# FFN-out of a hybrid decoder layer in one core: more units computed by Strassen products, operands loaded twice

## The chip, the core and the metric

One core of a Trainium2 chip runs the whole layer as one program. The engines are TensorE (PE, with its weight loads PEld shown apart), VectorE (DVE), ScalarE (ACT), GpSimd (POOL) and SyncE (SP, which here only issues transfers). The metric is the device time of one execution in microseconds (us). The time before is 2707.65 us, the median of three runs (2701.99 to 2710.27).

## The reference, cut to what matters

The layer takes x of 512 tokens by 2048 channels in float32. The part that the change is about is the feed-forward block and what follows it:

```python
h = rmsnorm(x, ffn_norm_g[i])
hid = h @ w_ffn_in[i]                                  # 2048 -> 2 x 5632
x = x + (silu(hid[..., :5632]) * hid[..., 5632:]) @ w_ffn_out[i]   # 5632 -> 2048
x = x + sigmoid(rmsnorm(x, ple_norm_g[i]) @ w_ple_gate[i]) * (p[i] @ w_ple[i])
```

Before it stand the combined projection, gated spatial mixing, stick-breaking attention and the output projection w_o.

## The kernel before

**Numbers.** Each float32 operand is split in a high part (rounded by ACT) and a low part (DVE subtracts the high one), and a product takes three matmuls: high x high, high x low, low x high (mm3, L269 to L273).

**Units and columns.** An operand *unit* is 256 channels by 512 tokens: two halves of the channels by two halves of the tokens, four blocks of [128, 256]. An output *column* (called a pair in the code, L744) is 256 channels by 512 tokens. A unit is multiplied in one of two ways.

- Plain (P): four weight blocks by two token rows, 12 matmuls of 512 columns.
- Strassen (S): seven products by sums of blocks (PRODUCTS, L52), 21 matmuls of 256 columns. It needs seven operand blocks (three as they are, four sums) and seven weight blocks (three and four in the same way). Outputs are mixed from PSUM by ACT and DVE (mix, L646). Two S units whose weights lie side by side share their weight preparation (a *double*, L402); a unit left over is a *single*.

In the stage before, FFN-in, the products are doubled: the high and low operand parts stand side by side, so that an S unit is 7 matmuls of 512 and 7 of 256 columns (L620 to L632). FFN-out does not use this.

**Weights.** A ring of four landing places and three slots (whi, wlo) holds them. For a P double one transfer of 512 KB is issued by SP (L314). For an S double SP issues 256 KB (the first block twice, L316) and 384 KB (L318), then POOL issues 256 KB that are added onto what has landed (L338); DVE adds two more sums (L350), ACT makes the high parts of 5 + 2 blocks (L334), DVE the low parts (L331). A landing place goes to the next weights once the low parts are made, so SP's issue of weights goes at the pace of DVE.

**The order.** Python emits the program unit by unit; a clock ticks once per P unit and twice per S double (tick, L198). At a tick a first load of a coming operand may be issued (fetch, at most one, among the next three), a form may be begun, and waiting steps go on. Manual dependencies hold what a tick emits in its place among the units.

**FFN-out.** The hidden vector is 22 units in DRAM. They don't fit at once, so there are three passes, each over all eight output columns (L1347): 8, 7 and 7 units, of the kinds in PASSES (L33), SSSSSPPP, SSSSSPP and SSSPPPP. The first pass writes its columns to DRAM as sums, the second adds to them (loads and stores 512 KB per column), the third adds, scales, adds the residual x1, writes x2, and sums squares for the next norm. In a pass's first column all units are multiplied plainly, since a plain product needs only the four blocks themselves. After the last column use of a unit its place is free for the next pass.

**Late forms.** An S operand that comes from DRAM is built by late_form (L509) and plain_first (L487): one load of 512 KB, the four blocks split, and at once the four sums, which stay in 4 KB of scratch per partition; one block's sum takes the place of a plain block and so waits until the plain column has used it. The gate stage after FFN-out (GATE = SSSSSPPP over x2) and FFN-in (over x1) use the same forms. There are eight places for S operands.

Of the kernel before, what the change touches and what calls it, by code (L numbers as in the profile page):

```python
# [32 lines left out]
PASSES = "SSSSSPPP", "SSSSSPP", "SSSPPPP"  # L33
# [18 lines left out]
PRODUCTS = (1, 0), (5, 5), (4, 1), (3, 4), (0, 6), (2, 2), (6, 3)  # L52
# [13 lines left out]
def hybrid_layer(  # L66
# [120 lines left out]
    builds = deque()  # L187
# [10 lines left out]
    def tick():  # L198
# [70 lines left out]
    def mm3(ps, sh, sl, mh, ml, start, stop, halved=False):  # L269
        for s in (slice(0, 256), slice(256, T)) if halved else (slice(None),):  # L270
            nc.tensor.matmul(ps[:, s], sh, mh[:, s], start=start, stop=False)  # L271
# [148 lines left out]
    class Form(Staged):  # L420


        def __init__(self, kind, steps, sizes, ready, src=None, far=False):
# [3 lines left out]
            self.src, self.there, self.block, self.due = src, not far, None, 0  # L427

# [6 lines left out]

        def raw(self):
# [3 lines left out]
        def get(self):  # L440
            if self in builds:
                builds.remove(self)
            return super().get()
# [43 lines left out]
    def plain_first(form, raw):  # L487
# [5 lines left out]
        for out, p, q, op in ((t[:, 0], b[:, 1], b[:, 0], ALU.subtract),  # L493
                              (v.f(), b[:, 1], b[:, 3], ALU.subtract),
                              (t[:, 1], t[:, 0], b[:, 3], ALU.subtract),
                              (t[:, 2], t[:, 1], b[:, 2], ALU.add)):
            nc.vector.tensor_tensor(out=out, in0=p, in1=q, op=op)  # L497
        give(raw)
        form.at_plain = True
        yield  # L500
# [5 lines left out]
        split_into(x[:, 1, 0], x[:, 1, 1], v.f())  # L506
        give(v)

    def late_form(src, ready=always, gain=None, far=False):  # L509
# [3 lines left out]
        def steps(form):  # L513
# [5 lines left out]
            yield from plain_first(form, w)  # L519
            return form.operand()  # L520

        return Form("S", steps, [(parts, 2 * PLACE, "place")] + [(wholes, 1024, "low")] * 2, ready,
                    src, far)

    def strassen_form(src, ready=always, gain=None, raw=PLACE):


        def steps(form):
            w = src()
            form.blocks = (parts.take(2 * PLACE, "place"),)  # L530
            if gain:
# [3 lines left out]
            nc.vector.tensor_tensor(out=b[:, 4], in0=b[:, 1], in1=b[:, 0], op=ALU.subtract)  # L535
            nc.vector.tensor_tensor(out=b[:, 1:6:4], in0=b[:, 1:5:3],
                                    in1=b[:, 3:4].to_broadcast([P, 2, 256]), op=ALU.subtract)
# [950 lines left out]
```

## Time and profile before

| | |
|---|---|
| median of three runs | 2707.65 us |
| the profiled execution | 2701.99 us, of which the span from first to last instruction is 2701.9 us |
| FFN-in, 44 columns | about 1175 to 2047 us in the span |
| FFN-out, passes 1, 2, 3 | about 2049 to 2214, 2214 to 2364, 2364 to 2510 us |
| gate stage | about 2520 to 2702 us |
| DVE, ACT, POOL busy over the span | 79%, 51%, 17% |

The stages' edges are read from the matmuls: in FFN-out an S unit shows as matmuls of 256 columns and a P unit as matmuls of 512. The views used are the profile's page, groups of instructions by line and shape within a stretch, windows (busy time of each engine in a stretch, granted clock, busy share of the 16 DMA engines), waits, the timeline, and the transfers of one tensor. A mean duration of an instruction includes the time in which the next one has already begun, so for matmuls the pace is taken from windows and not from durations.

### The profile page before, as it was taken

The numbers are of one execution on the slowest core, as the hardware profiler recorded it, in microseconds if no ns is written. First come the engines' busy times: TensorE is split into PE (matmuls) and PEld (weight loads), VectorE is DVE, ScalarE is ACT, GpSimd is POOL, SyncE is SP. The second block draws the span as 40 slices with busy tenths as digits, with TensorE's granted clock in tenths as the row PEclk, the third lists the DMA queues.
The fourth block names the chain that finished last, engine by engine and source line by source line (L and its number), as shares of the span: only waits on it lengthen the run. The fifth ranks groups of instructions, "written<-read, shape, count | busy, mean of one in ns | idle before, by whom it ended". The sixth has DMA issues, their size and how long they took to land.

```text
span 2701.9 us, 43167 instructions
## 1 busy us (share of the span) xinstructions
PE 2668.1 (99%) x15875; PEld 2354.6 (87%) x15875; DVE 2147.0 (79%) x3621; ACT 1367.3 (51%) x2143; POOL 459.0 (17%) x543
## 2 busy tenths in 40 slices
PE   8999999999999999999999999999999999999999
PEld 6888888989998889988888888888888999988898
DVE  7687878787887566688988888888889667688776
ACT  7656565655554343374444444444445344453543
POOL 0232323232220000001111111111111111110110
PEclk9999999999999999999999999999999999999999
DMA  7677777777776467678888888888887668688784
GB/s 224 156 185 175 181 173 186 170 187 197 177 186 197 140 173 200 173 219 211 212 212 202 200 203 205 201 198 210 195 210 206 181 167 262 184 249 236 218 243 133
DMA packets 303268, 529.40 MB, mean 196 GB/s; under 512 B 25680, under 2 KB 162896, under 8 KB 303056
## 3 DMA queue, kind: packets, MB, share of 16 engines
q1 hardware_dynamic: 242304, 426.22, 49.9%
q0 software_dynamic: 60752, 100.43, 23.8%
q8 instruction: 124, 2.03, 0.3%
q14 instruction: 88, 0.72, 0.1%
HBM read 479.36 MB, written 47.19 MB: 195 GB/s over the span
## 4 chain that ended last, share of the span: by engine, by line
PE 88%; DVE 5%; DMA 2%; ACT 2%; issue 1%; POOL 1%; SPq 0%; DVEq 0%; ACTq 0%; POOLq 0%
PE ps L629 39%; PE ps L272 14%; PE ps L273 14%; PE ps L271 14%; PE small L629 4%; DVE wlo L331 2%; DVE out L688 1%; PE small L1084 1%; PE small L959 1%; ACT whi L334 1%; DMA wholes<-w_in 0%; DMA wholes<-w_first 0%; DVE wholes L350 0%; PE small L1034 0%; DVE parts L267 0%
## 5 line engine op out<-in xcount | busy, mean ns | idle before, releaser
L334 ACT ACTIVATE whi<-wholes 128x512 fp32r<-128x512 f32 (+4 forms) x950 | 857.6, 917 | 838.3 <-DVE wholes L350 261.9
L629 PE MATMUL ps<-parts,whi 128*128 128x512 f32 x3384 | 1134.8, 398 | 0.3 <-DVE p L688 0.3
L331 DVE TENSOR_TENSOR wlo<-wholes,whi 128x512 fp32r<-128x512 f32 (+4 forms) x950 | 962.4, 1046 | 101.0 <-ACT whi L334 100.5
L271 PE MATMUL ps<-parts,whi 128*128 128x256 f32 (+1 forms) x2675 | 855.1, 323 | 15.7 <-ACT parts L266 9.7
L272 PE MATMUL ps<-parts,whi 128*128 128x256 f32 (+1 forms) x2640 | 857.0, 325 | 1.0 <-DVE parts L267 0.8
L273 PE MATMUL ps<-parts,wlo 128*128 128x256 f32 (+1 forms) x2640 | 855.9, 325 | 0.9 <-DVE wlo L331 0.9
L629 PEld LDWEIGHTS ps<-parts,wlo 128*128 128x128 f32 x3384 | 635.8, 188 | 142.6 <-issue 1.0
L629 PE MATMUL ps<-parts,wlo 128*128 128x256 f32 x3384 | 671.1, 279 | 0.0
L271 PEld LDWEIGHTS ps<-parts,whi 128*128 128x128 f32 x2675 | 508.8, 190 | 60.7 <-ACT parts L266 10.8
L629 PEld LDWEIGHTS ps<-parts,whi 128*128 128x128 f32 x3384 | 545.3, 189 | 5.0 <-issue 1.0
L272 PEld LDWEIGHTS ps<-parts,whi 128*128 128x128 f32 x2640 | 502.7, 191 | 47.2 <-DVE parts L267 2.8
L273 PEld LDWEIGHTS ps<-parts,wlo 128*128 128x128 f32 x2640 | 502.7, 191 | 41.2 <-DVE wlo L331 2.8
L350 DVE TENSOR_TENSOR wholes<-wholes 128x256 f32<-128x256 f32 (+1 forms) x794 | 326.8, 412 | 21.8 <-DMA wholes<-w_ffn_out 4.0
L338 POOL DMA_DIRECT2D wholes<-w_ffn_in x172 | 149.7, 871 | 693.0 <-DVE wholes L350 238.8
L688 DVE TENSOR_TENSOR out<-out,ps 128x256 f32<-128x256 f32 x388 | 160.3, 415 | 131.7 <-ACT out L685 131.5
L338 POOL DMA_DIRECT2D wholes<-w_in x132 | 118.0, 895 | 486.1 <-DVE wholes L350 145.7
L655 DVE TENSOR_TENSOR out<-out 128x256 f32<-128x256 f32 x144 | 60.9, 423 | 114.7 <-ACT out L652 112.2
L629 PE MATMUL small<-parts,whi 128*128 128x512 f32 x344 | 136.5, 397 | 0.0
L267 DVE TENSOR_TENSOR parts<-wholes,parts 128x1024 fp32r<-128x1024 f32 (+4 forms) x131 | 123.7, 950 | 14.9 <-ACT parts L266 14.5
L266 ACT ACTIVATE parts<-wholes 128x1024 fp32r<-128x1024 f32 (+4 forms) x131 | 105.8, 834 | 42.0 <-DVE wholes L497 20.0
L338 POOL DMA_DIRECT2D wholes<-w_ffn_out x56 | 56.9, 1020 | 403.4 <-DMA wholes<-w_ffn_out 139.6
L1328 ACT ACTIVATE out<-out 128x512 f32<-128x512 f32 x44 | 27.8, 633 | 157.9 <-DVE out L1327 157.9
(121 smaller groups left out, 1655.0 us busy)
## 6 DMA issues: line engine op xcount, KB each, us to landing
wholes<-w_ffn_in SPq DMA_DIRECT2D x172, 384.0 KB, 5.6
wholes<-w_in SPq DMA_DIRECT2D x132, 384.0 KB, 4.9
wholes<-w_ffn_in SPq DMA_DIRECT2D x172, 256.0 KB, 4.8
wholes<-w_ffn_in POOLq DMA_DIRECT2D x172, 256.0 KB, 5.4
wholes<-w_in SPq DMA_DIRECT2D x132, 256.0 KB, 4.2
wholes<-w_in POOLq DMA_DIRECT2D x132, 256.0 KB, 5.0
wholes<-x SPq DMA_DIRECT2D x33, 512.0 KB, 5.5
wholes<-w_ffn_out SPq DMA_DIRECT2D x31, 512.0 KB, 4.5
```

The lines of the kernel that those rows point to most:

```text
L266: return (nc.scalar.activation(hi, src, AF.Copy), nc.vector.tensor_tensor(out=lo, in0=src, in1=hi.bitcast(F32), op=ALU.subtract))
L267: nc.vector.tensor_tensor(out=lo, in0=src, in1=hi.bitcast(F32), op=ALU.subtract))
L271: nc.tensor.matmul(ps[:, s], sh, mh[:, s], start=start, stop=False)
L272: nc.tensor.matmul(ps, sh, ml, start=False, stop=False)
L273: return nc.tensor.matmul(ps, sl, mh, start=False, stop=stop)
L331: in_turn(nc.vector.tensor_tensor(out=self.lo[:, blocks], in0=r, in1=h.bitcast(F32), op=ALU.subtract))
L334: in_turn(nc.scalar.activation(h, r, AF.Copy))
L338: nc.gpsimd.dma_start(out=raw[:, 3:5], in_=self.src[:, 1:3], accum_op=ALU.add)
L350: in_turn(nc.vector.tensor_tensor(out=o, in0=x, in1=y, op=ALU.add))
L629: m = nc.tensor.matmul(out, l, r, start=first and k == 0, stop=last and k == 1)
L655: in_turn(nc.vector.tensor_tensor(out=out, in0=x, in1=y, op=op))
L688: in_turn(nc.vector.tensor_tensor(out=out, in0=x, in1=y, op=op))
```

## The change

1. PASSES becomes the sizes 8, 7, 7. All 22 units of FFN-out are built as S operands. PLAIN_UNTIL says in how many first columns the unit at each place of a pass is still multiplied plainly: one column for places 0 to 3, two for places 4 to 7. All later columns of a pass are S throughout.
2. A late form no longer makes its sums from the first load. It splits the four plain blocks, gives the buffer back, and enters a new queue, seconds. A tick in which no form is begun issues the second load of the same 512 KB (into a buffer of five blocks); two ticks later DVE makes the sums in that buffer and they are split. If the unit has been used plainly for the last time by then, one step does all four sums; otherwise the one that replaces a plain block waits as before. Where there is a norm gain (x1, x2), ACT applies it again to the second load. If a unit is wanted as S earlier than that, its steps are emitted on the spot. While a used form waits for its second load, no first load of another is begun.
3. First loads of a pass's operands are queued at the last column of the pass before it (for the first pass: of FFN-in; for the gate: of pass 3). Before, the queue was open throughout.
4. The blocks and products are renumbered so that another sum sits in the shared place; PRODUCTS, the order of the weight blocks in memory and strassen_form follow. The counts of instructions per form and weight stay the same there. The form of the first projection keeps its sums from one load (all_first).

```diff
-PASSES = "SSSSSPPP", "SSSSSPP", "SSSPPPP"
+PASSES = 8, 7, 7
+PLAIN_UNTIL = 1, 1, 1, 1, 2, 2, 2, 2
...
-PRODUCTS = (1, 0), (5, 5), (4, 1), (3, 4), (0, 6), (2, 2), (6, 3)
+PRODUCTS = (1, 2), (5, 4), (4, 3), (3, 6), (0, 5), (2, 0), (6, 1)
...
         last, units = traced()[-1], dict(newest)
-        for f in list(builds)[:AHEAD]:
-            if not f.there and f.ready() and fits([(wholes, 1024, "old"), (wholes, 1024, "low")]):
+        urgent = [f for f in seconds if f.used]
+        for f in list(builds)[: 0 if urgent else AHEAD]:
+            if not f.there and f.ready() and fits([(wholes, 1024, "old")]):
                 f.fetch()
                 break
         if builds and builds[0].ready() and builds[0].arrived() and fits(builds[0].sizes):
             builds.popleft().step()
+        elif seconds and fits([(wholes, 5 * 256, "old")]):
+            (urgent or seconds)[0].fetch_second()
...
+        def fetch_second(self):
+            if self in seconds:
+                seconds.remove(self)
+            self.second, self.due_second = self.src(5 * 256), clock[0] + WAIT
+
+        def second_arrived(self):
+            if self.forced and self.second is None:
+                self.fetch_second()
+            return self.forced or (self.second is not None and clock[0] >= self.due_second)
...
+    def plain_first(form, raw, gain=None):
+        x = form.operand()
+        split_into(x[:, 0:4, 0], x[:, 0:4, 1], cut(raw.f()))
+        give(raw)
+        form.at_plain = True
+        seconds.append(form)
+        yield
+        while not form.second_arrived():
+            yield
+        w = form.second
+        b = cut(w.f())
+        if gain:
+            gained(w.f(0, 1024), w.f(0, 1024), *gain)
+            yield
+        tt(b[:, 4], b[:, 3], b[:, 2])
+        if form.used:
+            tt(b[:, 2:0:-1], b[:, 4:2:-1], twice(b[:, 1]))
+            tt(b[:, 3], b[:, 2], b[:, 0], ALU.add)
+            yield
+            split_into(x[:, 3:7, 0], x[:, 3:7, 1], b[:, 1:5])
+            give(w)
+            return
...
+    def plain_left(n, j, until=PLAIN_UNTIL):
+        return tuple(max(0, u - j) for u in until[:n])
...
-    hs = [spilled_form(k, "hid", u) for u, k in enumerate("".join(PASSES))]
-    builds.extend(hs)
+    hs = [spilled_form("S", "hid", u) for u in range(KH // 2)]
...
     for m in range(KH):
-        o = pair(fs, last=m == KH - 1, plain=m == 0, doubled=7).out()
+        if m == KH - 1:
+            builds.extend(hs[: PASSES[0]])
+        o = pair(fs, last=m == KH - 1, plain=(0 if m else 1,) * KU, doubled=7).out()
...
         for j in range(KU):
+            if j == KU - 1:
+                builds.extend(hs[at : at + PASSES[c + 1]] if c + 1 < len(PASSES) else gs)
...
-            pr = pair(units, last=j == KU - 1, plain=j == 0, at=first)
+            pr = pair(units, last=j == KU - 1, plain=plain_left(n, j), at=first)
```

More of the change, by code (lines that the diff above doesn't have):

```diff
@@ L518, in steps @@
             yield
-            yield from plain_first(form, w)
+            yield from plain_first(form, w, gain)
             return form.operand()
-        return Form("S", steps, [(parts, 2 * PLACE, "place")] + [(wholes, 1024, "low")] * 2, ready,
+        return Form("S", steps, [(parts, 2 * PLACE, "place")] + [(wholes, 1024, "low")], ready,
                     src, far)
```

92 lines of the change are left out of this document (58 added, 34 removed).

## The prediction, made before the changed kernel was run

> **What bounds the kernel now.** I read the page first, then PE's waits from 1190 us on, then windows of one kind of unit, then windows of 20 us over the pass starts.
>
> ```profile
> span 2701.9 us, 43167 instructions
> PE 2668.1 (99%) x15875; PEld 2354.6 (87%) x15875; DVE 2147.0 (79%) x3621; ACT 1367.3 (51%) x2143; POOL 459.0 (17%) x543
> q1 hardware_dynamic: 242304, 426.22, 49.9%
> q0 software_dynamic: 60752, 100.43, 23.8%
> ...
> PE ps L271 <- ACT parts L266: 4.7, 3, 2.5
> PE ps L271 <- ACT whi L334: 1.9, 2, 1.1
> PE ps L271 <- DVE out L688: 1.8, 1, 1.8
> ...
> 1300.00:2000.00 700.00, 700.00 (x4017) 610.72 (x4015) 619.88 (x1113) 336.10 (x468) 125.30 (x144) 1.00 0.82 203
> 2088.41:2096.63 8.22, 8.22 (x40) 6.81 (x38) 8.05 (x14) 3.71 (x4) 2.14 (x2) 1.00 0.62 155
> 2096.63:2109.22 12.59, 12.59 (x106) 12.59 (x105) 4.23 (x9) 4.04 (x6) 2.09 (x2) 1.00 0.72 191
> ```
>
> PE bounds it: few waits are left, and the longest ones in FFN-out are for the splitting of late operands (L266). In FFN-in (1300 to 2000) PE never idles although DVE is 619.88/700 = 89% busy and the DMA engines 82%; so these loads are borne. The last two windows are three P units and five S units of pass 1. A P unit takes 8.22/3 = 2.74 us, an S unit 12.59/5 = 2.518 us; an S unit saves 0.222 us.
>
> Beside the price stands PEld: busy for 6.81 of 8.22 us in P units, and for 12.59 of 12.59 in S units. By columns streamed (12 x 512 against 21 x 256) an S unit would save an eighth, 0.34 us; with every matmul bringing its own weight load, the load sets the pace. The Trainium skill (Perfetto Trace Analysis, Identifying the Most-Contended Engine) says that PE's headroom is judged by the busy share of weight loads and not by that of matmuls; the trace agrees, at 100%. By streamed columns alone the 53 units below would give 18.2 us instead of 11.8.
>
> ```profile
> 1170.00:1190.00 20.00, 18.75 (x88) 15.39 (x87) 16.23 (x30) 16.51 (x25) 1.95 (x2) 1.00 0.93 317
> 1190.00:1210.00 20.00, 20.00 (x95) 16.47 (x94) 18.83 (x35) 14.28 (x23) 4.35 (x5) 1.00 0.99 283
> 2040.00:2060.00 20.00, 18.19 (x83) 14.97 (x82) 19.81 (x40) 11.76 (x17) 1.73 (x2) 0.91 0.67 177
> 2060.00:2080.00 20.00, 18.09 (x94) 14.41 (x93) 16.58 (x27) 8.32 (x12) 3.02 (x3) 1.00 0.89 255
> 2240.00:2260.00 20.00, 19.68 (x139) 18.38 (x139) 13.54 (x25) 8.37 (x11) 2.98 (x3) 1.00 0.98 295
> 2380.00:2400.00 20.00, 18.26 (x104) 16.20 (x103) 13.49 (x20) 8.67 (x12) 2.13 (x2) 0.91 0.80 241
> 2520.00:2540.00 20.00, 16.37 (x87) 13.37 (x86) 15.31 (x24) 9.68 (x14) 4.18 (x5) 1.00 0.94 262
> 2540.00:2560.00 20.00, 19.68 (x105) 16.90 (x106) 13.48 (x25) 11.01 (x18) 1.74 (x2) 0.91 0.67 188
> ```
>
> These are the starts of FFN-in, pass 1, 2, 3 and the gate. Lost is PE's idle time, and 0.09 x 20 = 1.8 us wherever the granted clock falls to 0.91. Pass 1: 1.81 + 1.91 + 1.8 = 5.5 us; pass 2: 0.3; pass 3: 1.74 + 1.8 = 3.5; gate: 3.63 + 0.32 + 1.8 = 5.8; FFN-in 1.25. Together 16 us that the change may win or double.
>
> **The change part by part.** *More S units.* Outside the first columns, P units number 3, 2 and 4 per column over seven columns, 63; afterwards only the second columns keep 4 + 3 + 3 = 10. So 53 units change, 53 x 0.222 = **-11.8 us**, if PE stays the bound.
>
> *DVE and DMA in pass 3.* This pass loads and stores most.
>
> ```profile
> 2418.04:2492.01 73.97, 73.97 (x449) 66.47 (x448) 63.35 (x94) 32.50 (x44) 8.54 (x8) 1.00 0.82 238
> 2229.00:2249.00 20.00, 20.00 (x121) 17.75 (x120) 18.13 (x32) 9.05 (x13) 3.68 (x4) 1.00 1.07 346
> ...
> L331 DVE TENSOR_TENSOR wlo<-wholes,whi 128x1024 fp32r<-128x1024 f32 x9 | 11.0, 1217 | 0.0
> L655 DVE TENSOR_TENSOR out<-out 128x256 f32<-128x256 f32 x17 | 7.2, 421 | 0.3
> L331 DVE TENSOR_TENSOR wlo<-wholes,whi 128x1280 fp32r<-128x1280 f32 x4 | 6.0, 1488 | 1.9 <-ACT whi L334 1.9
> L733 DVE TENSOR_TENSOR out<-ps,out 128x512 f32<-128x512 f32 x8 | 5.4, 686 | 3.0 <-PE ps L273 3.0
> L350 DVE TENSOR_TENSOR wholes<-wholes 128x256 f32<-128x256 f32 x8 | 3.4, 426 | 0.3
> L331 DVE TENSOR_TENSOR wlo<-wholes,whi 128x512 fp32r<-128x512 f32 x4 | 2.7, 684 | 0.0
> L497 DVE TENSOR_TENSOR wholes<-wholes 128x256 f32<-128x256 f32 x4 | 1.6, 415 | 0.0
> L267 DVE TENSOR_TENSOR parts<-wholes,parts 128x1024 fp32r<-128x1024 f32 x1 | 1.2, 1215 | 0.0
> L267 DVE TENSOR_TENSOR parts<-wholes,parts 128x768 fp32r<-128x768 f32 x1 | 0.9, 948 | 0.0
> ...
> wholes<-w_ffn_in SPq DMA_DIRECT2D x172, 384.0 KB, 5.6
> wholes<-w_ffn_in SPq DMA_DIRECT2D x172, 256.0 KB, 4.8
> wholes<-w_ffn_in POOLq DMA_DIRECT2D x172, 256.0 KB, 5.4
> wholes<-w_ffn_out SPq DMA_DIRECT2D x31, 512.0 KB, 4.5
> ```
>
> The first window is four columns of pass 3: 63.35/4 = 15.84 us of DVE per column of 18.49. Two P doubles become S doubles: each 1.488 + 2 x 0.426 + 0.684 - 1.217 = +1.81. Two adds of 512 (L733) become one of 256 and one of 512, -0.26. The operand work in the window (1.6 + 1.2 + 0.9, a quarter each: 0.93) leaves. Sum 18.3 us by full durations; if the added ones overlap as those in FFN-in do without costing PE, less, and the lower bound is PE's own 7 x 2.518 = 17.63. So 0 to 0.6 us per column.
>
> DMA: the SP queue moved 426.22 MB in 49.9% of 2701.9 us, 0.316 MB/us; the POOL queue 100.43 MB in 23.8%, 0.156. An S double is 640 KB and 256 KB, 2.07 + 1.68 = 3.75 us of all 16 engines; a P double 512 KB, 1.66. A column now takes 0.82 x 18.49 = 15.2, less about 0.4 for one gate operand, plus 2 x 2.09: 18.9 us against 17.63, a share of 1.07. That is just what 2229 to 2249 reached (1.07, 346 GB/s, no idle of PE), over 20 us only. If 1.07 holds, 0; if 1.00 is the most that lasts, 18.9 - 17.63 = 1.3 us per column. Six columns: 0 to 7.7 us. I take **+3.5**, DVE included, in the middle, since both engines stand at the edge and neither is clearly over. Passes 1 and 2 have no such lack: fewer transfers, and DVE without scaling, residual and norm.
>
> The Trainium skill (DMA: Bandwidth & Descriptors, Specifications) gives about 358 GB/s from HBM per core; a pass 3 column would move 7 x 448 KB + 3 x 512 KB = 4.78 MB in 17.63 us, 271 GB/s, which by that ceiling would not bind at all. The trace had its engines at 1.07 with 346 GB/s, with fewer of the adding transfers; no run here shows 358. By it the +3.5 would be 0.
>
> *Pass 1's start.* Now the last FFN-in column carries four forms' splits and sums, 4 x (1.215 + 4 x 0.415 + 0.948) = 15.3 us of DVE on top of a column that is at 89%; DVE shows 19.81 of 20, and PE waits for its mixing (L688). In the built order of the changed kernel, five first splits stand there, 6.1 us; the sums come in the next two columns. Most of the 5.5 goes: **-4.5** (-5.5 to +2, if the fourth operand's second half comes late).
>
> *Pass 2's start.* The same, with nothing to win: **+0.5** (0 to 4).
>
> *Pass 3's and the gate's late halves.*
>
> ```profile
> L479 SPq DMA_DIRECT2D wholes<-hid x22: 320/327/528, 1240.6 to 2381.5; - x22
> DMA to landing us min/median/max: 2.3/5.2/8.0
> ...
> L266 ACT ACTIVATE parts<-wholes 128x1024 fp32r<-128x1024 f32 x13 | 13.7, 1052 | 1.8 <-DMA wholes<-hid 1.5
> L483 ACT ACTIVATE wholes<-wholes,gcol 128x512 f32<-128x512 f32 x10 | 6.7, 714 | 2.2 <-DMA wholes<-x 2.2
> ```
>
> A second half takes 5.2 landing, 2 x 0.415 + 0.69 of sums (the middle one like L733), 1.05 high, 1.22 low: 9.0 us; 11.8 with the longest landing. At pass 3, in the built order, the third unit's second load stands after the last P double of the first column and is wanted one single S unit later: 5.48 + 2.52 = 8.0 us of cover. Late by 1 to 3.8, and a fall of the clock with it, 1.8. DVE is full there too: five late forms' sums and splits (2 x 1.215 + 1.52 = 3.95 each) fall into two columns of 37 us. From 3.5 now to about 6: **+2.5** (0 to +8). What waits behind it on DVE is the low parts of the next weights, since DVE works in order.
>
> At the gate the norm gain is applied again, 2 x 0.714, so 10.4 us. The second loads of its third, fourth and fifth unit stand in the second column itself, up to half a double (2.5 us) before use. If SP runs a double (5 us) ahead, each is late by about 3; two such waits and a fall of the clock are 8 to 9 against 5.8 now, where late first halves cost it (those come earlier now): **+3** (-4 to +9).
>
> *FFN-in's start.* Eight more loads of 512 KB, 8 x 1.66 = 13.3 us of the engines, where they are at 0.93 and 0.99 for 40 us. Weights and second halves queue behind them: **+3.5** (0, if they slide to where FFN-in leaves 18% free, to 11). The fetches that bunch in each last column I cost at nothing, since the P weights behind them are the light ones (1.66 against 3.75) and are needed 20 us later; without that cover, 10 us, as in rival two.
>
> Sum: -11.8 + 3.5 - 4.5 + 0.5 + 2.5 + 3 + 3.5 = **-3.3 us**. Against the profiled execution's 2701.99 that is 2698.7; the median lies 5.7 higher, so 2707.65 - 3.3 = **2704 us**.
>
> **The rivals.** 0.3% is 8.1 us, about what a measurement of this kernel can tell from no change; faster is below 2699.5, slower above 2715.8.
>
> *One: the late halves are really hidden.* Sums off the last column, eight plain units as cover: pass 3 and gate starts lose half of their 9.3 us (-4.6 instead of +5.5), the transfers hold at 1.07, FFN-in's start is unharmed: -11.8 - 4.5 + 0.5 - 4.6 = -20, hence 2687. For it: 2229 to 2260 with share 1.0 and only 0.3 us idle. Against: the short covers above.
>
> *Two, slower: pass 3 becomes bound by transfers.* If the engines give 1.00 and no more, its columns pay 7.7 us, and the last columns' bunched loads (six of the gate, 6 x 1.66 = 10 us) find no gap: 17.7 in place of 3.5, hence 2704 + 14.2 = 2718; with FFN-in's start at its upper end, 2726. It decides from a lasting share of 1.0 on. For it: 1.07 was seen for 20 us only. Against: PE did not wait then.
>
> *Three: all-Strassen columns don't pay.* Today P units follow the S products and hide their mixing. Without them a column's last add waits on the last product, and 18 columns that lose 0.5 us each (an add of 0.42 to 0.69) give back 9: 2713. Against: FFN-in's columns are all S and lose nothing, 700.00 of 700.00.
>
> **How the numbers follow.** Forecast 0.45 (own range 2694 to 2715), one 0.25, two 0.23, three 0.07. Faster: most of one (0.24) and a part of the forecast (0.07), 0.31. Slower: most of two (0.18), 0.05 of the rest, 0.23. Within: 0.46. The range cuts half of one's lower side and the upper end of two: 2685 to 2726.
>
> **What would show it.** S windows of FFN-out at 2.52 us per unit with PEld full; the windows of pass 3 at DMA 1.0 or more and DVE above 0.95, with waits of PE on wlo and whi; second halves (L267, L266) as releasers at the starts of pass 3 and the gate; a full clock at 2040 to 2060. Wrong would make it an unbroken PE in pass 3 (rival one), or losses of more than 1 us per column there (rival two).

## The result, and the profile after

The changed kernel takes 2723.48 us (median of 6 runs, 2721.07 to 2725.51), beside 2706.52 us (2698.29 to 2710.82) for the kernel before in the same rounds: 1.0066 times as long, 95% interval 1.0053 to 1.008. It is slower, by 17.0 us; 2704 us had been forecast, 3.3 less than before. One run of the last version tried below, at a mean granted clock of 0.65, took 3719.6 us and is left out of its median.

First the page of the changed kernel, the lines that answer to those of before.

```profile
span 2722.2 us, 44416 instructions
PE 2668.2 (98%) x16334; PEld 2374.5 (87%) x16334; DVE 2204.5 (81%) x3685; ACT 1405.6 (52%) x2174; POOL 477.3 (18%) x566
```

PE is busy for 2668.2 us; it was 2668.1. So the span is longer by 20.3 us in which PE idles, and the busy time, which should have fallen by the 11.8 us of the unit price, did not fall, because some of it ran at half the clock (below).

Where this happened is read from windows that end at the stages' own marks. In the changed kernel these are changes of the matmuls' width. Before, a pass ended in P units and the next began with them, so its edge is taken 3, 2 and 4 units of 2.74 us behind the last change (2213.3, 2362.5 and 2509.1); the edges given with the time before (2214, 2364, 2510) lie near these changes and leave out the last P units. Columns: the stretch, its length, then busy time (and instructions) of PE, weight loads, DVE, ACT, POOL, the granted clock, the DMA share and GB/s. Before: passes 1, 2, 3 and the gate.

```profile
2049.00:2221.50 172.50, 170.55 (x1090) 154.88 (x1091) 115.18 (x196) 72.94 (x97) 21.88 (x22) 0.99 0.68 188
2221.50:2367.97 146.47, 146.15 (x996) 135.80 (x994) 108.56 (x188) 62.76 (x88) 19.24 (x19) 1.00 0.78 224
2367.97:2520.06 152.09, 150.35 (x869) 133.37 (x868) 125.91 (x184) 69.17 (x90) 15.78 (x15) 0.99 0.78 234
2520.06:2701.90 181.84, 172.65 (x1124) 157.51 (x1122) 131.05 (x205) 76.63 (x103) 21.33 (x21) 0.99 0.71 199
```

The same four stages of the changed kernel:

```profile
2054.70:2220.40 165.70, 164.46 (x1240) 158.40 (x1240) 131.52 (x209) 80.02 (x96) 22.61 (x26) 1.00 0.84 241
2220.40:2363.80 143.40, 143.40 (x1089) 138.50 (x1088) 121.02 (x199) 68.17 (x89) 25.21 (x26) 1.00 0.92 264
2363.80:2524.30 160.50, 150.13 (x1090) 143.29 (x1089) 143.67 (x228) 76.19 (x98) 25.39 (x26) 0.97 0.90 263
2524.30:2722.20 197.90, 179.03 (x1125) 160.08 (x1123) 144.80 (x221) 90.40 (x120) 23.04 (x22) 0.96 0.69 201
```

Before, pass 1 began after a wait of 1.8 us, the one for DVE out that the prediction shows; it is counted to the pass here, so FFN-in ended at 2047.2 and pass 1 took 174.3. The price is 0.222 us for each of the 17, 11 and 25 units that became Strassen units.

| stage | before | after | difference | unit price | the rest | forecast of the rest |
|---|---|---|---|---|---|---|
| end of FFN-in | 2047.2 | 2054.7 | +7.5 | | +7.5 | +3.5 |
| pass 1 | 174.3 | 165.7 | -8.6 | -3.8 | -4.8 | -4.5 |
| pass 2 | 146.5 | 143.4 | -3.1 | -2.4 | -0.7 | +0.5 |
| pass 3 | 152.1 | 160.5 | +8.4 | -5.6 | +14.0 | +3.5 and +2.5 |
| gate | 181.8 | 197.9 | +16.1 | | +16.1 | +3 |
| sum | 2701.9 | 2722.2 | +20.3 | -11.8 | +32.1 | +8.5 |

These are single traces. In seven runs below whose FFN-in is the same code as the changed kernel's, FFN-in ends between 2054.9 and 2059.2, so at this place a difference below some 4 us is not told apart, and 7.5 is at the low end. Pass 3, where its code is unchanged, repeats within 0.5 us.

Passes 2 and 3 now have the same products in the same order, seven units a column. Pass 2 takes 143.4 us without one idle moment of PE; pass 3 takes 17.1 us more. That comparison inside one execution needs no price: what pass 3 has beside its products costs 17.1 us. Smaller windows say where; the changed kernel again, FFN-in's start, pass 1's start, then pass 2's first two columns, pass 3's first, second and other columns, and the gate's first columns:

```profile
1180.00:1205.00 25.00, 23.82 (x105) 19.68 (x106) 18.88 (x34) 21.04 (x32) 4.58 (x5) 0.93 0.99 310
1205.00:1225.00 20.00, 17.40 (x85) 14.65 (x84) 17.76 (x30) 16.09 (x22) 2.60 (x3) 0.91 0.86 256
2050.00:2070.00 20.00, 20.00 (x96) 16.80 (x95) 18.75 (x30) 11.21 (x15) 1.72 (x2) 1.00 0.91 298
...
2220.40:2258.00 37.60, 37.60 (x208) 32.70 (x207) 33.18 (x54) 18.92 (x22) 3.48 (x4) 1.00 0.89 276
2363.80:2382.90 19.10, 19.10 (x87) 15.80 (x86) 14.07 (x21) 8.49 (x10) 3.03 (x3) 1.00 0.97 286
2382.90:2413.40 30.50, 22.38 (x122) 19.83 (x121) 24.17 (x42) 12.03 (x16) 3.03 (x3) 0.89 0.75 230
2413.40:2524.30 110.90, 108.65 (x884) 107.66 (x883) 105.43 (x167) 55.67 (x73) 19.34 (x20) 0.98 0.93 267
2524.30:2547.00 22.70, 17.80 (x69) 13.38 (x68) 19.38 (x25) 14.69 (x20) 5.59 (x6) 0.89 0.97 290
2547.00:2570.00 23.00, 20.22 (x114) 16.62 (x112) 16.50 (x29) 15.07 (x22) 2.09 (x2) 0.96 0.75 233
2570.00:2591.40 21.40, 15.77 (x74) 12.83 (x75) 15.65 (x25) 10.84 (x13) 1.75 (x2) 0.84 0.71 223
```

Pass 2's first two columns take 37.6 us, pass 3's 19.1 + 30.5 = 49.6: 12.0 lost, all in the second column. The other six columns take 110.9, and pass 2's six 143.4 - 37.6 = 105.8: 5.1 lost, most of it one wait of 2.2 us and the fall of the clock behind it. Pass 1's start runs at full clock, as foretold. PE's waits after 1150 us are for:

```profile
PE ps L280 <- ACT parts L270: 10.4, 6, 3.5
PE ps L281 <- DVE parts L271: 10.3, 9, 3.3
PE ps L692 <- ACT out L789: 2.6, 1, 2.6
```

Nearly all are the splits of operands (L270, L271; L266, L267 before), 20.7 us together, where they had 5.4 us before (4.7 for high parts, 0.7 for low ones). None is long: fifteen waits, the longest 3.5 us. Low clocks add to them. Each window's length times one minus its clock gives the loss: 1.8 + 1.8 in FFN-in's start, 3.4 and 2.2 in pass 3, 2.5 + 0.9 + 3.4 in the gate, 16 us in all; before it was three times 1.8.

*Why pass 3's second column waits.* The SP queue's issues of the second loads for pass 3's first three operands (rows left out between them):

```profile
2372.49 0.78 SPq L500 DMA_DIRECT2D wholes<-hid  x1
...
2375.15 0.43 SPq L500 DMA_DIRECT2D wholes<-hid  x1
...
2383.53 0.32 SPq L500 DMA_DIRECT2D wholes<-hid  x1
```

The landing times of the first and the second of them, one answer for each, and a window over that time:

```profile
DMA to landing us min/median/max: 9.3/9.3/9.3
...
DMA to landing us min/median/max: 10.3/10.3/10.3
...
2372.00:2382.00 10.00, 10.00 (x46) 8.27 (x45) 5.17 (x10) 2.95 (x4) 0.91 (x1) 1.00 1.05 318
```

DVE and PE behind them, from their timelines, with the idle time before the row in brackets:

```profile
2381.89 1.61 DVE L509 TENSOR_TENSOR wholes<-wholes 128x256 f32<-128x256 f32 x3 [3.44 <-DMA wholes<-hid]
2383.42 2.09 DVE L340 TENSOR_TENSOR wlo<-wholes,whi 128x1280 fp32r<-128x1280 f32 x2
...
2387.20 1.22 DVE L271 TENSOR_TENSOR parts<-wholes,parts 128x1024 fp32r<-128x1024 f32 x1
```

```profile
2384.64 0.50 PE L280 MATMUL ps<-parts,whi 128*128 128x256 f32 x2 [1.24 <-ACT parts L270]
2388.48 0.58 PE L281 MATMUL ps<-parts,whi 128*128 128x256 f32 x1 [3.33 <-DVE parts L271]
```

The first load leaves 10.4 us before the column's first Strassen product (2382.89), and the product that needs its sums follows three matmuls later. It lands after 9.3 us, in a stretch in which the DMA engines' share is 1.05; DVE idles 3.44 us for it. From the landing to the product that waits for the sums another 6.6 us pass, since DVE, in order, first makes low parts of the next weights (2383.42) and the second operand's sums. So the chain from issue to product is 2388.48 - 2372.49 = 16.0 us; the prediction had 9.0. And the third load leaves at 2383.53, 0.6 us *after* the column began. It leaves where DVE's first three sums end (2381.89 + 1.61 = 2383.50): SP waited for a landing place that these sums gave back. In the built program the third load's place shares 256 floats with that of the first operand's second load, a block that only the sums read. SP's waits from 2379 to 2384 agree, first for a landing and then for the sums:

```profile
SPq L500 <- DMA wholes<-hid: 2.3, 1, 2.3
SPq L500 <- DVE wholes L509: 1.7, 1, 1.7
```

The column's other wait, 2.91 and then 0.64 us, is for the third operand's sums, but no longer for its landing (4.5 us, at 2388.0). In the built order its last sum stands on DVE behind the first sum of the fourth operand, and DVE idles for that one's landing; the fourth load had left at 2391.36, when the split of the second operand gave its place back. DVE, then PE:

```profile
2398.43 0.76 DVE L509 TENSOR_TENSOR wholes<-wholes 128x256 f32<-128x256 f32 x2 [2.38 <-DMA wholes<-hid]
...
2400.34 0.62 PE L280 MATMUL ps<-parts,whi 128*128 128x256 f32 x3 [2.91 <-ACT parts L270]
```

So the 12.0 us are 4.6 of waits for the first operand, 3.6 for the third, and 3.4 of low clock behind them.

In FFN-in the same thing happens through another engine. ACT's timeline:

```profile
1211.80 1.34 ACT L504 ACTIVATE wholes<-wholes,gcol 128x512 f32<-128x512 f32 x2 [2.71 <-DMA wholes<-x]
...
1216.90 0.57 ACT L789 ACTIVATE out<-ps 128x512 f32<-128x512 f32 x1
```

The gain on a second load (L504) stands idle for 2.71 us for its landing, and the copy out of PSUM (L789) that PE needs stands behind it in ACT's order; PE waits 2.6 us for it, and the clock falls.

### The profile page after: what moved, and what is told of

Its sections match the earlier page's. It is cut to its first block, busy times and chain, and to the rows that moved or that the text cites. A ratio compares the mean times of both kernels' runs of the same rounds, so it can differ in the third digit from the quotient of the medians.

```text
span 2722.2 us, 44416 instructions
## 1 busy us (share of the span) xinstructions
PE 2668.2 (98%) x16334; PEld 2374.5 (87%) x16334; DVE 2204.5 (81%) x3685; ACT 1405.6 (52%) x2174; POOL 477.3 (18%) x566
## 4 chain that ended last, share of the span: by engine, by line
PE 86%; DVE 6%; DMA 3%; ACT 2%; issue 2%; POOL 1%; SPq 0%; DVEq 0%; ACTq 0%; POOLq 0%
PE ps L692 40%; PE ps L281 13%; PE ps L282 13%; PE ps L280 13%; PE small L692 4%; DVE wlo L340 2%; DVE parts L271 1%; DVE out L751 1%; DMA wholes<-hid 1%; DMA wholes<-x 1%; PE small L1158 1%; ACT whi L343 1%; PE small L1033 1%; DVE wholes L509 1%; PE small L1108 1%
## 5 line engine op out<-in xcount | busy, mean ns | idle before, releaser
L343 ACT ACTIVATE whi<-wholes 128x1280 fp32r<-128x1280 f32 (+3 forms) x960 | 876.1, 927 | 805.6 <-DVE wholes L359 273.7
L340 DVE TENSOR_TENSOR wlo<-wholes,whi 128x1280 fp32r<-128x1280 f32 (+3 forms) x960 | 984.3, 1059 | 86.5 <-ACT whi L343 86.0
L281 PE MATMUL ps<-parts,whi 128*128 128x256 f32 (+1 forms) x2799 | 881.2, 315 | 11.1 <-DVE parts L271 10.8
L280 PE MATMUL ps<-parts,whi 128*128 128x256 f32 (+1 forms) x2782 | 869.5, 315 | 21.3 <-ACT parts L270 15.7
L282 PE MATMUL ps<-parts,wlo 128*128 128x256 f32 (+1 forms) x2799 | 878.6, 315 | 0.6 <-DVE wlo L340 0.6
L692 PEld LDWEIGHTS ps<-parts,wlo 128*128 128x128 f32 x3384 | 635.8, 188 | 142.0 <-issue 1.0
L281 PEld LDWEIGHTS ps<-parts,whi 128*128 128x128 f32 x2799 | 536.5, 192 | 51.7 <-DVE parts L271 15.1
L280 PEld LDWEIGHTS ps<-parts,whi 128*128 128x128 f32 x2782 | 531.3, 192 | 57.2 <-ACT parts L270 18.5
L282 PEld LDWEIGHTS ps<-parts,wlo 128*128 128x128 f32 x2799 | 535.6, 192 | 33.1 <-DVE wlo L340 2.5
L692 PEld LDWEIGHTS ps<-parts,whi 128*128 128x128 f32 x3384 | 546.7, 189 | 9.8 <-ACT out L789 3.0
L359 DVE TENSOR_TENSOR wholes<-wholes 128x256 f32<-128x256 f32 (+1 forms) x840 | 348.2, 415 | 24.2 <-issue 3.5
L347 POOL DMA_DIRECT2D wholes<-w_ffn_in x172 | 149.7, 870 | 698.9 <-DVE wholes L359 261.5
L347 POOL DMA_DIRECT2D wholes<-w_in x132 | 118.4, 898 | 489.3 <-DMA wholes<-w_in 112.6
L271 DVE TENSOR_TENSOR parts<-wholes,parts 128x1024 fp32r<-128x1024 f32 (+4 forms) x126 | 132.3, 1058 | 25.2 <-ACT parts L270 25.0
L347 POOL DMA_DIRECT2D wholes<-w_ffn_out x79 | 74.1, 939 | 403.3 <-DMA wholes<-w_ffn_out 152.6
L270 ACT ACTIVATE parts<-wholes 128x1024 fp32r<-128x1024 f32 (+4 forms) x126 | 113.7, 920 | 51.0 <-DVE wholes L509 35.9
```

What stands on the lines that cost most here:

```text
L270: return (nc.scalar.activation(hi, src, AF.Copy), nc.vector.tensor_tensor(out=lo, in0=src, in1=hi.bitcast(F32), op=ALU.subtract))
L271: nc.vector.tensor_tensor(out=lo, in0=src, in1=hi.bitcast(F32), op=ALU.subtract))
L280: nc.tensor.matmul(ps, sh, mh, start=start, stop=False)
L281: nc.tensor.matmul(ps, sh, ml, start=False, stop=False)
L282: return nc.tensor.matmul(ps, sl, mh, start=False, stop=stop)
L340: in_turn(nc.vector.tensor_tensor(out=self.lo[:, blocks], in0=r, in1=h.bitcast(F32), op=ALU.subtract))
```

## The experiments

Durations of stages are from each run's own trace, between the same marks. The theory at first: the second loads, where they are applied at FFN-in and the gate, and their cover at pass 3, cost what was lost.

**The gate's operands from one load.** Forms over x2 take their sums from the first load, in the manner of before; FFN-in and FFN-out stay as changed.

```diff
-            yield from plain_first(form, w, gain)
+            yield from (all_first(form, w) if one else plain_first(form, w, gain))
...
+        how = {"one": n in ('x2',)} if kind == "S" else {}
...
```

> The gate's five Strassen operands (over x2) again make their sums from the first load; all else as in the changed kernel (2723.5 us). Theory A, late second halves are what the gate's start lost (16 us more than before from 2524 to the end): 2708 to 2712, and the waits of PE on the parts' splits between 2524 and 2592 fall from 13 us of idle to the 4 or 5 of the kernel before. Theory B, pass 3 hands on its full transfer engines and DVE, and the first loads that bunch in its last column: the gate still loses, 2719 to 2724.

2716.72 us (2712.93 to 2719.81), 1.0038 times before (1.0025 to 1.005): between the two. The gate falls from 197.9 to 190.0, 7.9 of its 16.1 us. What is left are waits for first splits, the longest 5.2 us. So half of the gate's loss is the second loads'; the other half is that first halves come late. Their queue now opens at pass 3's last column, where before three of the gate's operands were loaded in its third to fifth columns; and pass 3's seven Strassen operands would leave one of the eight operand places free for them, where before three were free.

**FFN-in's and the gate's operands from one load.**

```diff
+        how = {"one": n in ('x1', 'x2')} if kind == "S" else {}
...
```

> As the run with the gate from one load, and FFN-in's eight operands (over x1) from one load too. Theory A: FFN-in's start loses its wait of 2.6 us on ScalarE's copy and the clock's fall, 7 us in all, so 2702 to 2705, which leaves pass 3's start alone. Theory B (eight more loads do not matter, since the transfer engines were at 0.93 to 0.99 there in the kernel before too): within 3 us of the gate-only run.

2721.40 us, 1.0055 (1.004 to 1.007): neither theory's time came out. FFN-in ended at 2053.1, only 1.6 earlier than in the changed kernel's trace, pass 2 (146.2) and pass 3 (163.8) lost 6.1 more, and the gate (193.4) gained 4.5. The steps of these forms stand one turn of the order later than before; the run with FFN-out alone changed, below, takes this turn back and ends FFN-in at 2048.1. The extra transfers alone therefore don't explain FFN-in's 7.5 us.

**Every unit of FFN-out plain in the second column too.**

```diff
-PLAIN_UNTIL = 1, 1, 1, 1, 2, 2, 2, 2
+PLAIN_UNTIL = 2, 2, 2, 2, 2, 2, 2, 2
```

> All units of FFN-out are plain in the first two columns of a pass instead of the last four only. Price 12 units x 0.222 = +2.7 us. Theory A: each second half has a whole column (18 us) more, pass 3's start gives back 8 to 12 of its 12 lost, so 2714 to 2718. Theory B (pass 3 is short of DVE and transfers as a whole, and its first columns only show it): the wait moves to the third column, 2722 to 2728.

2719.28 us, 1.0046 (1.0031 to 1.0061), between the two. Pass 3 takes 157.1 instead of 160.5, though four more of its units pay 0.222 us. The waits moved to the third column, the longest 3.8 us: a longer cover helps, and the work behind it is still not done in time.

**The gate's third to fifth unit plain in its second column.**

```diff
+GATE_UNTIL = 1, 1, 2, 2, 2, 1, 1, 1
...
-            plan(w_gate[j], GATE if j else "P" * KU)
+            plan(w_gate[j], kinds_of(GATE, j, GATE_UNTIL))
...
-            o = pair(gs, plain=(0 if j else 1,) * KU).out()
+            o = pair(gs, plain=plain_left(KU, j, GATE_UNTIL)).out()
```

> The gate's third to fifth unit are plain in its second column too. Price 3 units x 0.22 = +0.7 us. Theory A: the second loads that stand in that column get a column of cover, 8 to 12 us back, 2712 to 2716. Theory B: the gate waits anyway, for x2 and weights that come late, 2720 to 2725.

2713.61 us, 1.0027 (1.0016 to 1.0038); the gate takes 186.5, 11.4 less. Theory A held. Three units that use the cheaper product one column too early cost 0.67 us to put off, and cost 11.4 where they are not.

**FFN-out alone changed: FFN-in and the gate as before.** One load, the turns of before, and the gate's operands open from pass 3's start.

```diff
+        how = {"one": n in ("x1", "x2")} if kind == "S" else {}
...
+        if c == len(PASSES) - 1:
+            builds.extend(gs)
...
-                builds.extend(hs[at : at + PASSES[c + 1]] if c + 1 < len(PASSES) else gs)
+                builds.extend(hs[at : at + PASSES[c + 1]] if c + 1 < len(PASSES) else ())
```

> FFN-in's and the gate's operands are built just as before (one load, same ticks, the gate's queue open through pass 3); only FFN-out is changed. The run with both from one load had one tick more in each form and still waited 3 us at FFN-in's start. Theory A, late operands at the stage starts: FFN-in ends where it did before (2047 against 2055), 7 us back; the gate, whose operands now find one free place in pass 3 where there were three, lies between the 190 us of the gate-only run and the 182 of the kernel before, 185 to 188. Total 2705 to 2709. Theory B, the transfers and DVE of pass 3 are handed on: the gate stays at 189 or more, total 2711 to 2716.

2714.07 us, 1.0031 (1.0019 to 1.0044). FFN-in ends at 2048.1, and the gate takes 187.0, both as theory A had it; pass 3 takes 168.1, which it had not, and the total lies in theory B's band. Together pass 3 and the gate take 355.1 us, 358.4 in the changed kernel and 333.9 before. The all-Strassen pass itself brings the loss, whichever of the two stages shows it.

**What binds pass 3's later columns.** Two runs, each with one thing added per column from the third on. Another load of the residual (512 KB):

```diff
+            if x1 and j > 1:
+                nc.sync.dma_start(out=x1.f(0, 1024), in_=spill["x1", j])
```

> The changed kernel, with one more transfer of 512 KB in each of pass 3's columns 2 to 7. Now these six columns take 110.9 us. Theory B, the 16 transfer engines bind there: each of them pays 1.66 us, 119 to 121 us. Theory A, they do not bind, only operands that come late at the starts do: 110 to 113 us.

Or one more operation of 1024 columns on DVE:

```diff
+                if j > 1:
+                    nc.vector.tensor_tensor(out=x1.f(), in0=x1.f(), in1=x1.f(), op=ALU.max)
```

> The changed kernel, with one more DVE instruction of 1024 columns (1.22 us, 1.15 where it follows without a gap) in each of pass 3's columns 2 to 7. If DVE binds these columns (its windows show 96 to 100%), six of them pay 7 us, 117 to 119 us in place of 110.9. Theory A, DVE only looks full: 110 to 113 us.

The six columns took 110.9 us in the changed kernel, 113.3 with the loads, 121.6 with the operations. Windows of 76 us within them, of the changed kernel:

```profile
2430.00:2506.00 76.00, 73.75 (x595) 73.03 (x595) 72.97 (x119) 37.15 (x49) 15.47 (x16) 0.98 0.96 276
```

With the loads:

```profile
2430.00:2506.00 76.00, 72.57 (x582) 71.50 (x582) 71.02 (x114) 34.71 (x44) 14.59 (x15) 0.98 1.01 302
```

With the DVE operations:

```profile
2430.00:2506.00 76.00, 68.32 (x523) 67.26 (x523) 68.60 (x108) 31.38 (x42) 14.59 (x15) 0.93 0.88 246
```

Each of the two ran once. Six more transfers would cost 6 x 1.66 = 10 us if the transfers set the pace; they cost 2.4, 0.3 above theory A's band, with the DMA share at 1.01 for 76 us: the DMA engines have room left. Six operations of 1.22 us, 7.3 in all, cost 10.7, more than their own length. But that run added more than work. The operation needs nothing but the residual, so it stands in DVE's order 19 us or more ahead of the add that it was written before (2430.62 and 2449.99 in the third column), and DVE waits there for the residual's landing, which it never does in the changed kernel:

```profile
DVE wholes L1440 <- DMA wholes<-x: 6.3, 4, 3.8
```

So 7.3 + 6.3 = 13.6 us of DVE's time were taken and 10.7 of them came out, part of them as low clock (0.93), while DVE was busy for only 68.60 of 76 us. These columns can spare transfers and cannot spare DVE's time, which is 72.97 of 76 us busy in the changed kernel; that DVE's work as such sets the pace is not shown. Pass 2's columns, with the same products, point the same way:

```profile
2261.00:2336.00 75.00, 75.00 (x628) 75.00 (x627) 64.06 (x108) 34.42 (x47) 17.22 (x18) 1.00 0.99 267
```

PE never idles there at a DMA share of 0.99, above pass 3's 0.96, but with DVE busy for 64.06 of 75 us.

**Second loads given out earlier.** A turn of the order may begin an operand's step and also issue a second load.

```diff
-        elif seconds and fits([(wholes, 5 * 256, "old")]):
+        if seconds and fits([(wholes, 5 * 256, "old")]):
```

> As changed, but one turn of the order may begin a new operand and issue a second load; before, a turn that began a step left second loads waiting. In the order they then stand earlier: at FFN-in's start by one to three turns, in pass 3 by up to one (hid17's), at the gate by one to two. Theory A (the second loads are given out too late, in the order itself): FFN-in's start loses 3 instead of 7.4, pass 3 about 10 instead of 13.9, the gate 12 instead of 16: 2710 to 2716. Theory B (they stand early enough in the order; what delays them is the landing places, scratch buffers that DVE must give back first, and SP's queue that waits for these): every stage within 2 of the changed kernel's, 2719 to 2727.

2726.43 us, 1.0069 (1.0052 to 1.0086); FFN-in ends at 2056.3, pass 3 takes 161.5. No stage gains: theory B. An earlier place in the order is worth nothing here. The third load does leave earlier, 16.3 us after pass 3's start in place of 19.7; but the one that DVE's first sums wait for leaves later, after about 15 us in place of 8.7, and DVE idles 5.89 us for it.

**Second loads through the POOL queue.**

```diff
-            self.second, self.due_second = self.src(5 * 256), clock[0] + WAIT
+            self.second, self.due_second = self.src(5 * 256, nc.gpsimd), clock[0] + WAIT
...
```

> As changed, but the second loads of all operands go through the POOL queue instead of SP's; their number, size and place in the order stay. In pass 3's first column the POOL queue has no adding weight loads, so that they don't stand behind SP's weight loads that wait for DVE (23.2 us of such waits from 2340 to 2433). Theory A (SP's queue in order is what makes hid17's second half leave only at 2383.5, after its column began): it leaves before 2380, the 5.8 us in which DVE waits for these landings go, pass 3 takes 152 to 156 instead of 160.5, and the total is 2712 to 2718. Theory B (the landing places are not free before then, or POOL's queue waits behind its own adding loads): pass 3 159 to 164, total 2720 to 2728.

2737.89 us, 1.0111 (1.0096 to 1.0126), slower than either, beyond theory B's band. Pass 2 takes 150.8 us in place of 143.4, with one wait of 4.7 us for weights, pass 3 163.4 and the gate 200.6. POOL's timeline at pass 3's start (2370.3) says why, first an adding weight load (L347), then second loads (L500):

```profile
2383.96 0.93 POOL L347 DMA_DIRECT2D wholes<-w_ffn_out  x1 [5.46 <-issue]
2384.61 0.85 POOL L500 DMA_DIRECT2D wholes<-hid  x1
2386.19 0.55 POOL L500 DMA_DIRECT2D wholes<-hid  x1 [0.73 <-issue]
...
2394.58 0.55 POOL L500 DMA_DIRECT2D wholes<-hid  x1 [5.97 <-DVE wholes L509]
```

The first leaves 14.3 us after the pass's start, in place of 8.7. Against what was expected, the POOL queue has adding weight loads in this column, and the second loads stand behind one. So this run does not settle what SP's order costs the first two. The third waits 5.97 us for DVE's sums (L509), as it did on SP. So it is not SP's order that holds the third back, but its landing place.

**Is it room?** Two runs that leave the residual out of columns 0, 1 and 6 of pass 3. One leaves the load out too, so that its 1024 floats of scratch are free:

```diff
-            x1 = load(spill["x1", j]) if c == len(PASSES) - 1 else None
+            x1 = load(spill["x1", j]) if c == len(PASSES) - 1 and j not in (0, 1, 6) else None
...
```

> As changed, but columns 0, 1 and 6 of pass 3 leave the residual out: neither its load (512 KB, 1.66 us of the DMA engines) nor its add on DVE (1.22 us); the 1024 floats of scratch that it held from a column's start are free. In the order hid18's second load moves before the second column (it stood behind its start), and no operand is demanded before its second half has its turn. Only the first two columns of pass 3 are compared (49.6 us in the changed kernel, 37.5 without a wait). Theory A (the second halves are late because scratch is full, so that landing places come free only behind DVE's sums): 40 to 45. Theory B (scratch plays no part; DVE and landings are simply late): 46.5 to 49.6, the DVE work saved and no more.

The other loads and holds it, and leaves only DVE's add out:

```diff
-                nc.vector.tensor_tensor(out=h, in0=h, in1=x1.f(), op=ALU.add)
+                if j not in (0, 1, 6):
+                    nc.vector.tensor_tensor(out=h, in0=h, in1=x1.f(), op=ALU.add)
```

> The other half of the run without the residual: columns 0, 1 and 6 of pass 3 load the residual, and hold its scratch, as the changed kernel does, but leave its add on DVE out (1.22 us each). Theory A (room): the first two columns stay at 47 to 49.6, and the difference to the run without the load is the room's. Theory B (DVE's work is what is short): 43 to 46, as much as without the load.

Each ran once. The first column takes 19.1 us in both, without a wait. Pass 3's second and other columns without the load:

```profile
2385.40:2412.60 27.20, 21.14 (x123) 18.39 (x122) 23.91 (x46) 12.47 (x16) 3.03 (x3) 0.94 0.75 236
2412.60:2520.50 107.90, 106.96 (x884) 106.16 (x883) 103.13 (x162) 56.01 (x76) 19.34 (x20) 1.00 0.94 271
```

And without the add alone, the second column:

```profile
2384.40:2414.90 30.50, 23.50 (x123) 21.21 (x122) 23.28 (x41) 11.86 (x16) 3.03 (x3) 0.83 0.79 250
```

Without the add the first two columns take 49.6 us, as with it, but made up otherwise: PE idles 7.0 us in place of 8.1, and low clock takes 5.2 in place of 3.4. Without the load and its scratch they take 46.3, 3.3 less, with 6.1 us of idle and 1.6 of low clock; that is above theory A's 40 to 45 and 0.2 below theory B's band. In the built order of this run the third load shares no place with the first, and it leaves 6.7 us before the second column. PE then waits 0.21 and 0.64 us for the third operand, in place of 2.91 and 0.64 (2.23 without the add alone). The first operand's waits stay, 1.26 and 3.22 us, behind the 9.3 us of its own landing. So room is what the third operand lacked, and not the first; what the transfer left out adds to this is not told apart.

The other columns take 3.0 less too, so that the pass gains 6.3 of its 14.0 us. But the gate behind it takes 203.1, 5.2 more than in the changed kernel, with one wait of 12.08 us for a split; the two together take 357.2 us in place of 358.4. Whether that is the gate's own order in this run or what pass 3 hands on stays open.

**A version with two all-Strassen passes.** Pass 3 keeps its kinds of before, its operands and those of FFN-in and the gate come from one load as before, and pass 3's first loads open at pass 2's third column.

```diff
 PASSES = 8, 7, 7
+KINDS = "SSSSSSSS", "SSSSSSS", "SSSPPPP"
...
```

> Only passes 1 and 2 are all Strassen with two loads; pass 3 has the kinds and the single loads of before (SSSPPPP), FFN-in and the gate too; pass 3's first loads open in pass 2's third column. Theory A: pass 1 keeps its gain of 8.6 us (of which 3.8 are 17 units x 0.222 and the rest its lighter start), pass 2 its 3.1, pass 3 and the gate are as before: 2706 - 11.7 = 2693 to 2698. Theory B (all-Strassen columns before pass 3 load DVE and transfers so that the next stage pays): 2700 to 2706.

2697.64 us (median of seven runs, 2695.97 to 2704.48), 0.9976 times before (0.9965 to 0.9986): faster than both kernels, at the upper end of theory A's band. Its passes 1, 2, 3 up to the gate's second kind of work, and the rest:

```profile
2048.50:2212.20 163.70, 163.70 (x1238) 158.08 (x1237) 130.99 (x209) 80.05 (x96) 22.63 (x26) 1.00 0.85 243
2212.20:2356.90 144.70, 143.94 (x1089) 138.64 (x1088) 124.14 (x208) 68.73 (x90) 25.22 (x26) 1.00 0.89 256
2356.90:2513.00 156.10, 155.75 (x899) 137.44 (x898) 132.83 (x194) 70.49 (x92) 15.44 (x15) 1.00 0.81 244
2513.00:2694.60 181.60, 167.03 (x1096) 152.78 (x1094) 127.03 (x201) 76.59 (x103) 20.45 (x20) 0.96 0.67 190
```

(The third row ends at 2513.00, within the gate's first column.) Passes 1 and 2 keep what the change won there, at a granted clock of 1.00. Pass 3 and the gate together take 337.7 us, 3.8 more than before and 20.7 less than in the changed kernel.

## Why the prediction was wrong, step by step

**Where the sum went off.** Beside the unit price 8.5 us of loss had been forecast, and 32.1 came. Of the 23.6 us between them 13.1 are the gate's, 8.0 pass 3's and 4.0 FFN-in's; passes 1 and 2 gave 1.5 back. That 2723 lies between 2685 and 2726 is owed to the upper end, which was drawn for rival two; the forecast itself had the sign wrong.

**The unit price and the first two starts: right.** An S unit takes 105.8/42 = 2.52 us in pass 2, with weight loads busy throughout: 75.00 of 75.00 us from 2261 on. Hence rival three falls: 42 units without a P block lose nothing. Pass 1's start gave -4.8 for a forecast of -4.5, pass 2's -0.7 for +0.5, just below its bounds (0 to 4).

**"The third unit's second load stands after the last P double ... 8.0 us of cover" and "+2.5 (0 to +8)": the step that failed first.** It gave a price to the third unit's second half alone and put the first's at nothing. The first's load leaves 10.4 us before its column, and issue to product takes 16.0: PE waits 4.6 us for it and the clock falls once more. Two terms of the 9.0 us were mis-sized: 5.2 us of landing was 9.3 and 10.3 where last loads of one pass and second loads of the next meet (DMA share 1.05), and from landing to product 3.8 was 6.6, because DVE makes weights' low parts in between. The third's wait, 3.6 us, lies within the 1 to 3.8 that were named, but by luck: its load leaves 0.6 us after the column began and not a double ahead of its product, and it is covered by PE's own wait for the first. What the prediction left out there was the landing place, which the third load waits for; with that place free, in the run without the residual's load, the third's wait falls to 0.9 us. The start lost 12.0 us in place of 6 (the 3.5 of before and 2.5).

**"Two such waits and a fall of the clock ... +3 (-4 to +9)" at the gate: measured +16.1, outside its bounds.** This is the largest miss. The third to fifth unit were indeed late, as named, but with first halves late as well: -11.4 with these units put off, -7.9 with one load. The step that failed is the credit for first halves that "come earlier now". In the built order that holds for the fourth and fifth unit; the first three, which were loaded in pass 3's third to fifth columns, now come in its last column too, and with one load PE still waits 5.2 us for a first split.

**"The fetches that bunch in each last column I cost at nothing", with FFN-in's start at +3.5: half of it.** FFN-in lost 7.5, inside 0 to 11. It was put down to the engines' time for eight more loads; the run with one load and a turn more regained 1.6 of it, the one with the turns of before 6.6. With the 4 us by which FFN-in differs between traces the shares are not sharp, but order counts beside bytes, and the seen path was an in-order ACT that waited for a landing with a PSUM copy behind it.

**"+3.5, DVE included": 5.1 measured, of a size that was foreseen, and by the engine named second, as far as two single runs tell.** The prediction feared transfers. The added loads ran at a share of 1.01 over 76 us and cost a quarter of their time; 13.6 us of DVE's time, work and waiting, cost 10.7. Of the Trainium skill's figure of 358 GB/s per core (DMA: Bandwidth & Descriptors, Specifications) it was said that by it the transfers would not bind; 302 GB/s were held here without binding, and no window shown here reached the figure.

**Rival two** named 2718, up to 2726, and the result lies there. Its mechanism did not decide: transfers did not bind the pass. What it says of bunched loads in the last columns is nearer to what was found, but their price is paid in landings that come too late for one chain, not in engine time. **Rival one** is out: the covers were shorter than the pessimistic working had them. Of the 12.0 us at pass 3's start, room explains most of the third operand's wait; for the first, what the crowding of the transfers adds to its landing and what DVE's order adds behind it was not varied alone, and no run has a larger scratch.

## What to carry to other kernels

An operand that comes in two parts needs a place to land for each part, and the place can be one that the very engine that is behind gives back; count free buffers at the moment of issue before counting the microseconds of cover, and take landing times from the crowded stretch rather than the median. Where a late stage borrows slack (free operand places, light columns) from the one before it, a change that fills this slack must be judged at the later stage: here passes 1 and 2 gained, and pass 3's start and the gate lost more. Use the cheap product where the supply has room (passes 1 and 2), and keep the dear one where it buys time: the same idea in two of three passes is 0.24% faster.

## What the runs showed of the hardware

Most short waits cost nearly double. The two windows below, of the changed kernel, lie behind PE's waits of 3.3 us (2388) and 2.3 us (2542):

```profile
2388.50:2391.50 3.00, 3.00 (x14) 3.00 (x15) 2.98 (x5) 0.82 (x3) 2.17 (x2) 0.50 0.79 236
...
2543.00:2549.00 6.00, 6.00 (x20) 5.00 (x20) 3.37 (x9) 1.85 (x3) 2.91 (x2) 0.52 1.01 292
```

The clock stands at half, the first time for 3.4 us, the second for 6.8. Of the trace's 20.3 us 10.6 are this: 16 us of low clock after against 5.4 before. The Trainium skill (TensorE: Matmul & The Clock Gate, Why this matters for your kernels) warns of idle gaps over about 3 us; here a single wait of 1.8 us (pass 1 before) or 2.2 us (pass 3 after) was enough, so the measurement decides. It is not a rule without exception: in the run with added DVE operations a wait of 2.69 us, up to 2400.58, was followed by full clock, and so was one of 2.50 us.

```profile
2400.58:2406.27 5.69, 4.69 (x34) 4.24 (x35) 3.02 (x5) 3.00 (x4) 0.00 (x0) 1.00 0.47 148
```

As an estimate from these traces, a wait of about 2 us is to be priced at its length and mostly 1.7 us more, half of 3.4. The Trainium skill also says (Perfetto Trace Analysis, Optimization Strategy) that a gap that repeats on the engine that should be full can mean that there is no room for the next tile; the third operand's wait at pass 3's start, which went down from 3.6 to 0.9 us with its landing place free, is such a case, a single gap and not a repeating one.
